# A hybrid attention and RWKV-7 layer: the recurrence's chain, norm and outputs split by group, one PSUM bank per step, and a new program order

## The chip, the cores and the metric

The kernel runs on one core of one Trainium2 chip. The time is device microseconds of one execution; the median of three runs stands for the kernel before. The core's engines each run their own queue of instructions in order: TensorE (PE, with its weight loads PEld), VectorE (DVE), ScalarE (ACT), GpSimd (POOL), and SyncE (SP), which here only starts DMAs. They wait for each other by semaphores.

## The reference

One layer on x of 1024 tokens by 1024 features: a norm, one large projection, then multi-head latent attention (MLA, 4 heads) and an RWKV-7 recurrence (8 heads of 64) side by side, gates z, an output projection and a second norm. Cut to what matters:

```python
u = rmsnorm(h, norm_pre_g[l])
p = u @ w_in[l]
p_mla, p_rw, z = jnp.split(p, [MLA_COLS, MLA_COLS + RW_SHIFT_COLS], axis=-1)
c_q, c_kv, k_r = jnp.split(p_mla, [Q_LORA, Q_LORA + KV_LORA], axis=-1)
q = (rmsnorm(c_q, mla_q_norm_g[l]) @ mla_w_uq[l]).reshape(B, T, MLA_HEADS, MLA_NOPE + MLA_ROPE)
kv = (rmsnorm(c_kv, mla_kv_norm_g[l]) @ mla_w_ukv[l]).reshape(B, T, MLA_HEADS, MLA_NOPE + MLA_V)
...
def step(S, inp):
    r_t, w_t, k_t, v_t, kk_t, a_t = inp
    sa = jnp.einsum('bhvk,bhk->bhv', S, -kk_t)
    S = (S * w_t[:, :, None, :] + sa[..., None] * (kk_t * a_t)[:, :, None, :]
         + v_t[..., None] * k_t[:, :, None, :])
    return S, jnp.einsum('bhvk,bhk->bhv', S, r_t)
```

The state S of the recurrence (64 by 64 for each head) goes from token to token. The recurrence's output is normed by head, gets a bonus term, and is gated like the attention's output.

## The kernel before

The tokens are done in two halves of 512. The operations are letters with the half and, where there is one, the block behind them, and `PROGRAM` is their list. A is the first norm and the transposes of x (into uH and uL, a value split in two parts of reduced precision). X is the low-rank input of the decay and of a, and P the projections of one block of 128 columns (two heads) for r, k and v: 24 matmuls each, by `proj` (L209). E builds the block's chunk matrices. Z is the projection of one block of the gates, again 24 matmuls, and Y of two. M and T are the input of the latent attention: M projects (L532 to L534), copies the result out (L544, on DVE), norms it, and T transposes it, multiplies by the norm's gain (L559, DVE) and sends it to DRAM (cTd).

The recurrence is done by chunks of 64 tokens, 8 to a half. I inverts the chunks' triangular 64 by 64 matrices: on DVE, 31 steps of a product and an add (L417, L419) for the 32 by 32 blocks on the diagonal, then a round trip through DRAM (sx, st), then products on TensorE (L446, L453) for the block below. C is the chain over the 8 chunks. A step has four products: R = LS(first half of the columns) x S (L467), Y = LS(second half) x S (L470), U = AB x R (L479) and the new state from BK x U (L484), to which DVE adds the decayed old state SD (L490), and a second part of Y (L486). R and U are copied out of PSUM by ScalarE (L473, L481), Y too (L492); SD is made by POOL (L476). All four column blocks with both heads of each go through a step together, 8 small matmuls for a product (each two passes). N norms the output by head (L500 to L506; L502 and L503 are a logarithm and an exponential on ScalarE with a load of its tables each), and loads the bonus (bvd) onto the squares' place. G transposes the result (L518), applies gain and bias (L520) and writes it to DRAM (yrw).

The attention: B makes the cos and sin tables (L661 to L672), U loads the up weights (w_uq, w_ukv) and cTd and splits each value in two parts (L625 to L628), K turns the key's rope part, Q computes the rotated queries of 256 tokens (L750 and on), J the first head's q and k, `values` (L811 to L815) the values of two heads. S is attention for 4 heads (scores L834, probabilities times values L866) and the output projection (L912).

What sets the order: the kernel is handed to a list scheduler, in which the order of `PROGRAM` is the priority. The order that it builds is fixed on each engine. Buffers bind it: PSUM is allotted by tags, four banks of 512 numbers "pj" (projections), two "wk" and two "ch" (the chain, the norm's transposes, the attention's output). In SBUF a tag is one buffer, or as many as `bufs` says, shared by all that ask for it in turn: "q" has two. A tensor SV of the first kernel holds state and output of all four blocks of a half in one buffer; the values and the final output use its place later. LS, BK and AB come two blocks ("group") to a buffer, with two buffers.

Of the kernel before, what the change touches and what calls it, by code (L numbers as in the profile page):

```python
# [44 lines left out]
def layer(tc, x, pos, w_in, w_out, w_uq, w_ukv, vecs, w2, a2, consts, post_g, out):  # L45
# [84 lines left out]
    "A0 X0 P00 E00 Z00 P01 E01 Z01 P02 E02 Z02 P03 E03 I0 M0 Z03 Z04 Z05 C0 Z06 Z07 T0 A1 X1 N0",  # L130
    "P10 G0 E10 Z10 P11 E11 Z11 P12 E12 Z12 P13 E13 I1 M1 Z13 Z14 T1 Z15 Z16 Z17 C1 U B K Q0 Q1 Q2 Q3 J N1 G1 S",
# [3 lines left out]
def recurrence(tc, E):  # L135
# [17 lines left out]
    def stage_a(h):  # L153

        XT = (("v", "sq"), ("sg", "cs"), ("a", "k"), ("kf", "r"))
        for pr in range(2):
            xs = []
            for q in range(2):
                t = h * 4 + pr * 2 + q
                xh = [alloc(P1, (128, 512), XT[pr * 2 + q][i]) for i in range(2)]  # L160
                ss = alloc(P1, (128, 2), "ss1", bufs=4)
                for i in range(2):
                    SP.dma_start(xh[i], x[t * 128:(t + 1) * 128, i * 512:(i + 1) * 512])
                    junk = alloc(P1, (128, 512), "q", BF16, bufs=2)
                    S.activation(junk, xh[i], AF.Square, accum_out=ss[:, i:i + 1])
                G.tensor_tensor(ss[:, 0:1], ss[:, 0:1], ss[:, 1:2], ALU.add)
                E["rstd"](ss[:, 0:1], 1.0 / D)
                for i in range(2):
                    V.tensor_scalar(xh[i], xh[i], ss[:, 0:1], 1.0, ALU.mult, ALU.mult)
                xs.append(xh)  # L170
            for k2 in range(4):
                ps = pj((128, 2, 256))
                for kk in range(2):
                    kb = k2 * 2 + kk
                    for q in range(2):
                        PE.transpose(ps[:, kk, q * 128:(q + 1) * 128], xs[q][kb // 4][:, (kb % 4) * 128:(kb % 4 + 1) * 128], ident)  # L176
# [90 lines left out]

    def prep(h, xx, cb, gt):
# [48 lines left out]
        rk = alloc(P1, (128, 512), "q", bufs=2)  # L317
# [139 lines left out]
    def chain(h, gt):  # L457

        SV, Dg = gt["SV"], gt["Dg"]
        LS, BK, AB = ([gt["g"][b // 2][k][:, b % 2] for b in range(4)] for k in ("LS", "BK", "AB"))  # L460
        be = [(b, e) for b in range(4) for e in range(2)]
        for e in range(2):
            G.tensor_copy(SV[ev[e], 0, e], Sst[ev[e]])
        for c in range(NCH):
            pR = chp((128, 4, 64))
            for b, e in be:
                PE.matmul(pR[ev[e], b], LS[b][:, c, e, 0:64], SV[:, c, e, b], start=True, stop=True)  # L467
# [5 lines left out]
            S.copy(Rs, pR)  # L473
# [4 lines left out]
            for b, e in be:
                PE.matmul(pU[ev[e], b], AB[b][ev[e], c, 0:64], Rs[ev[e], b], start=True, stop=True)  # L479
            for e in range(2):  # L480
                S.copy(SV[ev[e], c, e], pU[ev[e]])  # L481
# [1 line left out]
            for b, e in be:
                PE.matmul(pS[ev[e], b], BK[b][:, c, e], SV[:, c, e, b], start=True, stop=True)  # L484
            for b, e in be:
                PE.matmul(pY[ev[e], b], AB[b][ev[e], c, 64:128], SV[ev[e], c, e, b], start=False, stop=True,  # L486
                          skip_group_check=True)
            for e in range(2):
                dst = SV[ev[e], c + 1, e] if c + 1 < NCH else Sst[ev[e]]
                V.tensor_tensor(dst, pS[ev[e]], SD[ev[e]], ALU.add)  # L490

            S.copy(SV[:, c, 0], pY)  # L492

    def group_norm(h, gt):

        y, sq = gt["SV"][:, :, 0], gt["SV"][:, :, 1]
# [6 lines left out]
        S.activation(ss, ss, AF.Exp, scale=-0.5)  # L503
        for c4 in range(0, NCH, 4):
            cs = slice(c4, c4 + 4)
            V.tensor_tensor(y[:, cs], y[:, cs], bc(ss[:, cs].unsqueeze(3), (128, 4, 4, 64)), ALU.mult)  # L506
        for e in range(2):
            for b in range(4):
                SP.dma_start(sq[ev[b % 2], :, (b // 2) * 2 + e], bvd[h, b, ev[e]].rearrange("p (c t) -> p c t", t=64))

    def outputs(h, gt):

        for g in range(2):
            for e in range(2):
                o = gt["SV"][:, :, 1, 2 * g + e]
                pT = chp((128, NCH, 64))
                for c in range(NCH):
                    PE.transpose(pT[:, c], gt["SV"][ev[e], c, 0, 2 * g:2 * g + 2].rearrange("p l v -> p (l v)"),  # L518
                                 ident[ev[e], ev[e]])
                V.scalar_tensor_tensor(o, pT, hln[:, 2 * g + e:2 * g + e + 1], o, ALU.mult, ALU.add)  # L520
                b = (2 * g + e) * 128
                SP.dma_start(yrw[b:b + 128, h * HALF:(h + 1) * HALF].rearrange("p (c t) -> p c t", t=64), o)

    def mla_in(h):
# [11 lines left out]
        for t in range(4):  # L536
# [7 lines left out]
            V.tensor_copy(cq, pss[t][:, 0:384])  # L544
# [6 lines left out]
    def mla_tail(h, cqs):  # L551
        for t, (cq, ss) in enumerate(cqs):
# [6 lines left out]
            V.tensor_tensor(cT, ps, bc(vec[:, V_QG:V_QG + 3].unsqueeze(2), (128, 3, 128)), ALU.mult)  # L559
# [42 lines left out]
    def op_m(h):  # L602
# [10 lines left out]
def attention(tc, E):  # L613
# [16 lines left out]
    identr = causalr = sint = cost = sintq = costq = None  # L630
    cqH = cqL = ckH = ckL = uqH = uqL = ukH = ukL = krT = None

    def op_b():
# [37 lines left out]

        V.tensor_scalar_mul(tabq, tab, -SCALE)  # L672

    def op_u():
# [17 lines left out]
        for kb in range(2):  # L692
            for i in range(2):
# [358 lines left out]
```

## Time and profile before

| | |
|---|---|
| median of the three runs | 796.23 us |
| the runs | 796.23, 797.51, 792.93 us |
| the profiled execution | 792.52 us |
| its span in the profile | 790.7 us (1.8 us lie around it) |
| mean granted TensorE clock | 0.93 |

A row of the timeline gives the start in us, the length, engine, line, operation, the tiles written and read, and how many instructions of a kind it holds; in brackets stands how long the engine had been idle before it and what released it. In a table of groups the busy time, the mean ns of one, and the idle time ahead stand behind the bars. A row of windows gives for each engine the busy time in that stretch and the count of instructions, in the order PE, PEld, DVE, ACT, POOL, then the granted clock of TensorE, the share of time in which DMA engines were busy, and GB/s. Line numbers in these rows are those of the kernel before.

### The profile page before, as it was taken

Reading aid. Unit: us, or ns where it says so; the run is one execution under the profiler, and the core shown is the slowest. Engines: PE = TensorE matmul, PEld = TensorE weight load, DVE = VectorE, ACT = ScalarE, POOL = GpSimd, SP = SyncE. Lnnn points to the kernel's source line nnn. Section 1 sums busy time; section 2 is a strip of 40 time slices with the busy share of each in tenths; the row PEclk is TensorE's granted clock in tenths of the full one; section 3 lists DMA queues with packets and bytes.
Section 4 is the critical chain, followed back from the end, with each engine's and each line's share of the span. In section 5 each row is a group of like instructions: output and inputs, shape, how many; then the busy total and the mean of one; then the engine's idle time right before and its main releaser. Section 6 shows DMA issues by size and latency. Waiting matters only on the chain.

```text
span 790.7 us, 13588 instructions
## 1 busy us (share of the span) xinstructions
PE 694.5 (88%) x5088; PEld 577.1 (73%) x5088; DVE 458.5 (58%) x888; ACT 346.3 (44%) x825; POOL 304.5 (39%) x426
## 2 busy tenths in 40 slices
PE   3699999997988998879999968597579998899996
PEld 2478787886866777658888856486469997788884
DVE  5464755759735420684685785484356766644342
ACT  6445455335534462444443532345435566532221
POOL 6443645627632444133455541112102237332110
PEclk9799999998979899869999989699879999999998
DMA  7323223262480123152233434502130034154321
GB/s 208 103 55 87 71 71 109 80 191 73 149 194 27 47 88 80 35 121 52 64 88 80 116 115 135 159 14 64 45 70 14 22 101 146 52 169 133 120 80 53
DMA packets 118818, 72.83 MB, mean 92 GB/s; under 512 B 47072, under 2 KB 108256, under 8 KB 118752
## 3 DMA queue, kind: packets, MB, share of 16 engines
q1 hardware_dynamic: 118752, 71.96, 32.3%
q8 instruction: 40, 0.66, 0.3%
q14 instruction: 26, 0.21, 0.1%
HBM read 54.38 MB, written 17.56 MB: 91 GB/s over the span
## 4 chain that ended last, share of the span: by engine, by line
PE 63%; DVE 14%; DMA 8%; ACT 5%; issue 4%; SPq 3%; POOL 3%; DVEq 0%; ACTq 0%; POOLq 0%
PE pj L209 23%; PE pj L912 11%; PE wk L358 4%; PE pj L834 4%; PE ch L866 3%; PE wk L372 3%; DVE XA L419 2%; DVE tmp L417 2%; PE wk L855 1%; PE pj L176 1%; PE pj L532 1%; PE pj L383 1%; PE ch L484 1%; SPq L436 1%; PE pj L785 1%
## 5 line engine op out<-in xcount | busy, mean ns | idle before, releaser
L209 PE MATMUL pj<-uH,w 128*128 128x512 f32 x672 | 226.6, 413 | 13.2 <-DVE st L559 6.6
L199 POOL TENSOR_TENSOR w<-wf,w 128x256 fp32r<-128x256 f32 x168 | 140.0, 865 | 147.9 <-ACT w L189 138.8
L209 PEld LDWEIGHTS pj<-uH,w 128*128 128x128 f32 x672 | 130.4, 196 | 45.0 <-DVE st L559 6.8
L209 PE MATMUL pj<-uL,w 128*128 128x512 f32 x336 | 137.0, 408 | 0.0
L209 PEld LDWEIGHTS pj<-uL,w 128*128 128x128 f32 x336 | 66.1, 197 | 15.2 <-issue 1.0
L189 ACT CAST w<-wf 128x1024 fp32r<-128x1024 f32 (+1 forms) x50 | 51.3, 1025 | 22.1 <-PE pj L534 11.2
L846 POOL TENSOR_SCALAR wf<-wf,sm 128x128 f32<-128x128 f32 (+7 forms) x32 | 24.2, 759 | 90.0 <-DVE sm L845 74.6
L476 POOL TENSOR_TENSOR SD<-SV,Dg 64x256 f32<-64x256 f32 x32 | 21.8, 680 | 45.8 <-DVE SV L490 38.4
L866 PE MATMUL ch<-BK,SV 128*128 128x256 f32 (+1 forms) x160 | 33.4, 292 | 4.2 <-ACT SV L814 3.9
L358 PEld LDWEIGHTS wk<-LS,pl 64*128 64x128 f32 x256 | 27.2, 194 | 11.1 <-issue 9.0
L970 DVE TENSOR_TENSOR SV<-pj,SV 128x512 f32<-128x512 f32 x16 | 11.1, 691 | 41.6 <-ACT cq L969 40.7
L197 POOL TENSOR_TENSOR w<-wf,w 128x224 fp32r<-128x224 f32 x32 | 23.0, 749 | 29.3 <-ACT w L189 29.3
L857 ACT CAST BK<-wk 128x512 fp32r<-128x512 f32 (+3 forms) x48 | 22.5, 484 | 26.9 <-PE wk L855 24.6
L358 PE MATMUL wk<-LS,pl 64*128 64x128 f32 x256 | 32.3, 292 | 1.5 <-DVE LS L316 1.5
L490 DVE TENSOR_TENSOR SV<-ch,SD 64x256 f32<-64x256 f32 x28 | 11.8, 421 | 37.7 <-PE ch L484 37.3
L842 ACT ACTIVATE wf<-pj,mx 128x512 f32<-128x512 f32 (+3 forms) x48 | 27.9, 587 | 11.5 <-DVE mx L839 8.1
L566 ACT ACTIVATE st<-pj 128x512 f32<-128x512 f32 x16 | 9.6, 598 | 52.1 <-PE pj L209 38.6
L858 DVE TENSOR_TENSOR AB<-wk,BK 128x512 fp32r<-128x512 f32 (+3 forms) x48 | 26.1, 551 | 9.6 <-ACT BK L857 9.1
L837 DVE TENSOR_REDUCE mx<-pj 128x1 f32<-128x512 f32 (+3 forms) x48 | 25.8, 550 | 9.0 <-PE pj L836 5.0
L866 PEld LDWEIGHTS ch<-BK,SV 128*128 128x128 f32 x160 | 27.1, 200 | 4.9 <-ACT SV L814 4.1
L417 DVE TENSOR_TENSOR tmp<-XA 128x31 f32<-128x31 f32 (+15 forms) x62 | 27.2, 439 | 4.3 <-DMA XA<-sa 2.8
L372 PEld LDWEIGHTS wk<-r,pl 64*128 64x128 f32 x256 | 26.7, 189 | 2.8 <-issue 2.8
(332 smaller groups left out, 1595.8 us busy)
## 6 DMA issues: line engine op xcount, KB each, us to landing
wf<-in_w_in_dram SPq DMA_DIRECT2D x42, 512.0 KB, 3.9
zs<-st SPq DMA_DIRECT2D x16, 256.0 KB, 2.7
wf<-in_x_dram SPq DMA_DIRECT2D x8, 512.0 KB, 3.8
out_dram<-SV SPq DMA_DIRECT2D x16, 256.0 KB, 2.0
wf<-in_w_in_dram SPq DMA_DIRECT2D x8, 448.0 KB, 3.6
bvd<-st SPq DMA_DIRECT2D x8, 256.0 KB, 2.0
SV<-bvd SPq DMA_DIRECT2D x16, 128.0 KB, 2.9
yrw<-SV SPq DMA_DIRECT2D x8, 256.0 KB, 2.4
```

The source lines that it names most:

```text
L189: S.copy(wh, wf)
L199: G.tensor_tensor(wl[:, sl], wf[:, sl], wh[:, sl].bitcast(F32), ALU.subtract)
L209: PE.matmul(ps, w_[:, kb], u_[:, kb], start=(n == 0), stop=(n == 23))
L358: PE.matmul(pE[e][:, ci], pl[r, c4 + ci, 1 - e:3 - e].rearrange("p a b -> p (a b)"), LS[r, c4 + ci, e, :], start=True, stop=True)
L372: PE.matmul(pB[:, c], pl[r, c, 1 - e:3 - e].rearrange("p a b -> p (a b)"), dD[r, c], start=True, stop=True)
L417: V.tensor_tensor(t3, bc(At[:, j, j + 1:32].unsqueeze(2), (128, n, w)), bc(X[:, j, 0:w].unsqueeze(1), (128, n, w)), ALU.mult)
L834: PE.matmul(s_, l_, r_, start=(n == 0), stop=(n == 4 and b1 < e))
L837: V.tensor_reduce(mx[:, n5:n5 + 1], s_, axis=AX.X, op=ALU.min)
L842: S.activation(pr[:, b0:b1], sc[:, 0:b1 - b0], AF.Exp, bias=mx[:, 0:1], scale=-1.0, accum_out=sm[:, n5:n5 + 1])
L858: V.tensor_tensor(PL[:, b0:b0 + nb, o], pt[:, 0:nb], PH[:, b0:b0 + nb, o].bitcast(F32), ALU.subtract)
L866: PE.matmul(py[:, o], l_, r_, start=(j == 0 and n == 0), stop=(j == nk - 1 and n == 2), skip_group_check=True)
L912: PE.matmul(po[nb], l_, r_[:, ns], start=(k0 == 0 and k == 0 and n == 0), stop=(k0 == 4 and k == 3 and n == 2), skip_group_check=True)
```

## The change

The order of the program is new. Inverse, chain, norm and outputs of a half stand ahead of M of that half, Z00 ahead of P00, B at the end of the first half, and J ahead of Q.

`chain`, `group_norm` and `outputs` get a group g of two blocks, and a half calls them once for each group. R, Y, U and the new state of a step stand in one PSUM bank, four quarters of it. SV is one tensor for each group, with two buffers. The norm's root is a power on POOL. M's copy and T's copy are ScalarE's; the gains of the two latent norms are multiplied onto the up weights instead (`scaled`). The scale of the queries, formerly in tables of its own, is applied where the rotated queries are split. The tag "q" has one buffer.

```diff
 PROGRAM = (
-    "A0 X0 P00 E00 Z00 P01 E01 Z01 P02 E02 Z02 P03 E03 I0 M0 Z03 Z04 Z05 C0 Z06 Z07 T0 A1 X1 N0",
-    "P10 G0 E10 Z10 P11 E11 Z11 P12 E12 Z12 P13 E13 I1 M1 Z13 Z14 T1 Z15 Z16 Z17 C1 U B K Q0 Q1 Q2 Q3 J N1 G1 S",
+    "A0 X0 Z00 P00 E00 Z01 P01 E01 Z02 P02 E02 Z03 P03 E03 I0 C00 C01 N00 G00 N01 G01 M0 Z04 Z05 Y06 T0 A1 X1 B",
+    "P10 E10 Z10 P11 E11 Z11 P12 E12 Z12 P13 E13 I1 C10 C11 N10 G10 N11 G11 M1 Z13 T1 Z14 Z15 Z16 Z17 U K J Q0",
+    "Q1 Q2 Q3 S",
 )
...
+            SV=alloc(P1, (128, NCH, 2, 2, 64), "SV", bufs=2),
         ) for _ in range(2)]
         return dict(
             g=gs,
-            SV=alloc(P1, (128, NCH, 2, 4, 64), "SV", bufs=1),
...
-        rk = alloc(P1, (128, 512), "q", bufs=2)
+        rk = alloc(P1, (128, 512), "q")
...
-    def chain(h, gt):
+    def chain(h, g, gt):
...
         for c in range(NCH):
-            pR = chp((128, 4, 64))
-            for b, e in be:
-                PE.matmul(pR[ev[e], b], LS[b][:, c, e, 0:64], SV[:, c, e, b], start=True, stop=True)
-            pY = chp((128, 4, 64))
...
+            pc = chp((128, 4, 2, 64))
+            pR, pY, pU, pS = (pc[:, i] for i in range(4))
+            for l, e in le:
+                PE.matmul(pR[ev[e], l], LS[:, l, c, e, 0:64], SV[:, c, e, l], start=(l == 0), stop=False,
                           skip_group_check=True)
-            Rs = alloc(P1, (128, 4, 64), "Rs")
+            for l, e in le:
+                PE.matmul(pY[ev[e], l], LS[:, l, c, e, 64:128], SV[:, c, e, l], start=False, stop=False,
+                          skip_group_check=True)
+            Rs = alloc(P1, (128, 2, 64), "Rs", bufs=2)
             S.copy(Rs, pR)
...
-    def group_norm(h, gt):
+    def group_norm(h, g, gt):
...
-        S.activation(ss, ss, AF.Ln, bias=epst[:, 1:2], scale=1.0 / 64)
-        S.activation(ss, ss, AF.Exp, scale=-0.5)
+        G.tensor_scalar(ss, ss, 1.0 / 64, GN_EPS, ALU.mult, ALU.add)
+        G.tensor_tensor(ss, ss, bc(E["mhalf"][:, 0:1].unsqueeze(2), (128, NCH, 2)), ALU.pow)
...
-            V.tensor_copy(cq, pss[t][:, 0:384])
+            S.copy(cq, pss[t][:, 0:384])
...
-            V.tensor_tensor(cT, ps, bc(vec[:, V_QG:V_QG + 3].unsqueeze(2), (128, 3, 128)), ALU.mult)
+            S.copy(cT, ps)
...
+    def scaled(dst_h, dst_l, src, c):
+
+        G.tensor_scalar(dst_h, src, vec[:, c:c + 1], 1.0, ALU.mult, ALU.mult)
+        V.scalar_tensor_tensor(dst_l, src, vec[:, c:c + 1], dst_h.bitcast(F32), ALU.mult, ALU.subtract)
...
-                split(uqH[:, kb, sl], uqL[:, kb, sl], wf)
+                scaled(uqH[:, kb, sl], uqL[:, kb, sl], wf, V_QG + kb)
...
-        V.tensor_scalar_mul(tabq, tab, -SCALE)
...
-        S.copy(qs[:, :, 0].bitcast(F32R), qo)
-        V.tensor_tensor(qs[:, :, 1], qo, qs[:, :, 0], ALU.subtract)
+        S.activation(qs[:, :, 0].bitcast(F32R), qo, AF.Copy, scale=-SCALE)
+        V.scalar_tensor_tensor(qs[:, :, 1], qo, -SCALE, qs[:, :, 0], ALU.mult, ALU.subtract)
...
-            vt = own[0][:, 2 * e:2 * e + 2].rearrange("p s (k c) -> p s k c", c=128)
+            vt = alloc(P2, (128, 2, 8, 128), "SV", F32R, bufs=2)
```

Three places show how the built order moves. In the rows a name is a tile with its number, `ch_4839` a bank of the chain, and the last field gives the columns of the result and the count.

On TensorE the end of the second half's chain, before: the last full step of all four blocks (LS_2658 and LS_2661 are its two groups).

```order
L467 MATMUL ch_4830<-SV_2664,LS_2658 64x64 x4
L467 MATMUL ch_4830<-SV_2664,LS_2661 64x64 x4
L470 MATMUL ch_4839<-SV_2664,LS_2658 64x64 x4
L470 MATMUL ch_4839<-SV_2664,LS_2661 64x64 x4
L479 MATMUL ch_4853<-Rs_4848,AB_2660 64x64 x4
L479 MATMUL ch_4853<-Rs_4848,AB_2663 64x64 x4
L486 MATMUL ch_4839<-SV_2664,AB_2660 64x64
L484 MATMUL ch_4864<-SV_2664,BK_2659 64x64 x4
L484 MATMUL ch_4864<-SV_2664,BK_2662 64x64 x4
L486 MATMUL ch_4839<-SV_2664,AB_2660 64x64 x3
L486 MATMUL ch_4839<-SV_2664,AB_2663 64x64 x4
```

The same place now: two of the second group's half-steps, one bank each (LS_2869 is the second group; the first group's steps stand ahead of these).

```order
L469 MATMUL ch_4625<-SV_2872,LS_2869 64x64 x4
L472 MATMUL ch_4625<-SV_2872,LS_2869 64x64 x4
L480 MATMUL ch_4625<-Rs_4634,AB_2871 64x64 x4
L485 MATMUL ch_4625<-SV_2872,BK_2870 64x64 x4
L487 MATMUL ch_4625<-SV_2872,AB_2871 64x64 x4
L469 MATMUL ch_4656<-SV_2872,LS_2869 64x64 x4
L472 MATMUL ch_4656<-SV_2872,LS_2869 64x64 x4
L480 MATMUL ch_4656<-Rs_4665,AB_2871 64x64 x4
L485 MATMUL ch_4656<-SV_2872,BK_2870 64x64 x4
L487 MATMUL ch_4656<-SV_2872,AB_2871 64x64 x4
```

A step of four blocks has become two of two blocks; the groups follow one another, and in both kernels no other matmul stands between the rows of this place.

On DVE, in the middle of the second half's inverse (tmp and XA are its operands), before:

```order
L544 COPY cq_4210<-pj_4056 128x384
L661 TENSOR_SCALAR q_4976<-xw_4978 128x256 x2
L419 TENSOR_TENSOR XA_3789<-XA_3789,tmp_3826 128x20x12
L662 TENSOR_SCALAR xw_4978<-q_4976 128x256
L544 COPY cq_4222<-pj_4057 128x384
L417 TENSOR_TENSOR tmp_3829<-XA_3789 128x247
L663 TENSOR_TENSOR q_4976<-q_4976,xw_4978 128x256
L419 TENSOR_TENSOR XA_3789<-XA_3789,tmp_3829 128x19x13
```

The same steps of the inverse now:

```order
L418 TENSOR_TENSOR tmp_3990<-XA_3953 128x240
L420 TENSOR_TENSOR XA_3953<-XA_3953,tmp_3990 128x20x12
L418 TENSOR_TENSOR tmp_3993<-XA_3953 128x247
L420 TENSOR_TENSOR XA_3953<-XA_3953,tmp_3993 128x19x13
L418 TENSOR_TENSOR tmp_3996<-XA_3953 128x252
L420 TENSOR_TENSOR XA_3953<-XA_3953,tmp_3996 128x18x14
```

The copies of M and the table work of B have left DVE's queue between the inverse's operations.

On TensorE near the start, where the low-rank products (L249, L250) wait for their input, before:

```order
L209 MATMUL pj_247<-uL_99,w_241 128x512
L209 MATMUL pj_247<-uH_98,w_241 128x512
L249 MATMUL pj_294<-xw_279,lora_228 128x512
L250 MATMUL pj_294<-xw_279,lora_228 128x512
L249 MATMUL pj_301<-xa_280,lora_228 128x512
```

And now (pj_293 is Z00's bank):

```order
L210 MATMUL pj_293<-uH_98,w_287 128x512 x2
L210 MATMUL pj_293<-uL_99,w_287 128x512
L210 MATMUL pj_293<-uH_98,w_287 128x512
L250 MATMUL pj_331<-xw_279,lora_228 128x512
L251 MATMUL pj_331<-xw_279,lora_228 128x512
L250 MATMUL pj_338<-xa_280,lora_228 128x512
```

The 24 matmuls of Z00 now stand between the input's projection (pj_247) and the low-rank products.

More of the change, by code (lines that the diff above doesn't have):

```diff
@@ L477, in chain @@
-            pU = chp((128, 4, 64))
-            for b, e in be:
-                PE.matmul(pU[ev[e], b], AB[b][ev[e], c, 0:64], Rs[ev[e], b], start=True, stop=True)
+                G.tensor_tensor(SD[ev[e]], SV[ev[e], c, e], bc(Dg[ev[e], :, c:c + 1], (64, 2, 64)), ALU.mult)
+            for l, e in le:
+                PE.matmul(pU[ev[e], l], AB[ev[e], l, c, 0:64], Rs[ev[e], l], start=False, stop=False,
+                          skip_group_check=True)
             for e in range(2):
                 S.copy(SV[ev[e], c, e], pU[ev[e]])
-            pS = chp((128, 4, 64))
@@ L483, in chain @@
[L483 to L487, printed above, removed]
+            for l, e in le:
+                PE.matmul(pS[ev[e], l], BK[:, l, c, e], SV[:, c, e, l], start=False, stop=False, skip_group_check=True)
+            for l, e in le:
+                PE.matmul(pY[ev[e], l], AB[ev[e], l, c, 64:128], SV[ev[e], c, e, l], start=False,
+                          stop=True, skip_group_check=True)
@@ L501, in group_norm, with outputs @@
             V.tensor_reduce(ss[:, cs], sq[:, cs], axis=AX.X, op=ALU.add)
-        S.activation(ss, ss, AF.Ln, bias=epst[:, 1:2], scale=1.0 / 64)
-        S.activation(ss, ss, AF.Exp, scale=-0.5)
+        G.tensor_scalar(ss, ss, 1.0 / 64, GN_EPS, ALU.mult, ALU.add)
+        G.tensor_tensor(ss, ss, bc(E["mhalf"][:, 0:1].unsqueeze(2), (128, NCH, 2)), ALU.pow)
         for c4 in range(0, NCH, 4):
             cs = slice(c4, c4 + 4)
-            V.tensor_tensor(y[:, cs], y[:, cs], bc(ss[:, cs].unsqueeze(3), (128, 4, 4, 64)), ALU.mult)
-        for e in range(2):
[L508 to L522, printed above, removed]
+            V.tensor_tensor(y[:, cs], y[:, cs], bc(ss[:, cs].unsqueeze(3), (128, 4, 2, 64)), ALU.mult)
+        for l in range(2):
+            for e in range(2):
+                SP.dma_start(sq[ev[l], :, e], bvd[h, 2 * g + l, ev[e]].rearrange("p (c t) -> p c t", t=64))
+    def outputs(h, g, gt):
+        SV = gt["g"][g]["SV"]
+        for e in range(2):
+            o = SV[:, :, 1, e]
+            pT = chp((128, NCH, 64))
+            for c in range(NCH):
+                PE.transpose(pT[:, c], SV[ev[e], c, 0].rearrange("p l v -> p (l v)"), ident[ev[e], ev[e]])
+            V.scalar_tensor_tensor(o, pT, hln[:, 2 * g + e:2 * g + e + 1], o, ALU.mult, ALU.add)
+            b = (2 * g + e) * 128
+            SP.dma_start(yrw[b:b + 128, h * HALF:(h + 1) * HALF].rearrange("p (c t) -> p c t", t=64), o)
     def mla_in(h):
@@ L606, in recurrence @@
         "A": stage_a, "X": op_x, "P": op_p, "M": op_m, "T": lambda h: mla_tail(h, cqs[h]),
-        "E": op_e, "I": lambda h: inverse(h, gts[h]), "C": lambda h: chain(h, gts[h]),
-        "N": lambda h: group_norm(h, gts[h]), "G": lambda h: outputs(h, gts[h]), "Z": lambda h, b: zgate(h, b, b + 1),
+        "E": op_e, "I": lambda h: inverse(h, gts[h]), "C": lambda h, g: chain(h, g, gts[h]),
+        "N": lambda h, g: group_norm(h, g, gts[h]), "G": lambda h, g: outputs(h, g, gts[h]), "Z": lambda h, b: zgate(h, b, b + 1),
         "Y": zgate2,
@@ L616, in attention @@
     alloc, bc = E["alloc"], E["bc"]
-    hln, epst, ident, causal, invf = (E[k] for k in ("hln", "epst", "ident", "causal", "invf"))
+    hln, epst, ident, causal, invf, vec = (E[k] for k in ("hln", "epst", "ident", "causal", "invf", "vec"))
     x, pos, w_out, w_uq, w_ukv, post_g, out = (E[k] for k in ("x", "pos", "w_out", "w_uq", "w_ukv", "post_g", "out"))
@@ L920, in op_s @@
     def op_s():
-        own.append(alloc(P2, (128, 4, T), "SV", F32R, bufs=1))
         prs, pp = {}, {}
@@ L951, in op_s @@
         load_wo(0, 2, "LS", 2, V, G)
-        po_ = alloc(P2, (128, 4, D), "SV", bufs=1)
-        pg = po_[:, 0]
+        sv = [alloc(P2, (128, 2, D), "SV", bufs=2) for _ in range(2)]
+        pg, *rows = (v_[:, i] for v_ in sv for i in range(2))
         SP.dma_start(pg, post_g.partition_broadcast(128))
@@ L964, in op_s @@
             ss = alloc(P2, (128, 2), "oss", bufs=2)
-            o = po_[:, 1 + t % 3]
+            o = rows[t % 3]
             for nb in range(2):
```

43 lines of the change are left out of this document (19 added, 24 removed).

## The prediction

> **What bounds the kernel now.** I read the page first (engine totals, the chain that ended last), then the waits of the tensor engine one by one on the timeline, and last the granted clock in windows.
>
> ```profile
> PE 694.5 (88%) x5088; PEld 577.1 (73%) x5088; DVE 458.5 (58%) x888; ACT 346.3 (44%) x825; POOL 304.5 (39%) x426
> ```
>
> The tensor engine works in 694.5 of 790.7 us, so 96 us of idling are what a change of order can win or lose. The other engines matter only where it waits for them. The largest such places that the change touches are these:
>
> ```profile
> 34.30 0.77 PE L249 MATMUL pj<-xw,lora 128*128 128x512 f32 x1 [6.01 <-DVE xw L241]
> 192.22 0.79 PE L209 MATMUL pj<-uH,w 128*128 128x512 f32 x1 [5.05 <-DVE cq L544]
> 231.03 0.48 PE L176 MATMUL pj<-cst,v 128*128 128x128 f32 x1 [3.33 <-DVE st L559]
> 468.53 0.79 PE L209 MATMUL pj<-uH,w 128*128 128x512 f32 x1 [6.60 <-DVE st L559]
> 510.26 0.74 PE L750 MATMUL pj<-pl,uH 128*128 128x256 f32 x4 [0.76 <-POOL pl L627]
> ```
>
> Each row gives the start, the length, the operation and, in brackets, how long the engine had stood idle and for what. In the second, third and fourth the engine waits for DVE copies (L544, L559) that stand in DVE's queue among the operations of the inverse. The last row is the start of the attention products that fill the second chain. Four steps of that chain stand bare, with nothing else on the tensor engine; one of them, by engine:
>
> ```profile
> 555.75 0.69 PE L467 MATMUL ch<-SV,LS 128*64 128x64 f32 x16 [0.53 <-DVE SV L490]
> 556.47 0.37 ACT L473 COPY Rs<-ch 128x256 f32<-128x256 f32 x1 [0.79 <-PE ch L467]
> 556.89 0.68 PE L479 MATMUL ch<-Rs,AB 64*64 64x64 f32 x16
> 557.68 0.76 ACT L481 COPY SV<-ch 64x256 f32<-64x256 f32 x2 [0.84 <-PE ch L479]
> 558.49 0.69 PE L484 MATMUL ch<-SV,BK 128*64 128x64 f32 x16
> 559.29 0.88 DVE L490 TENSOR_TENSOR SV<-ch,SD 64x256 f32<-64x256 f32 x2 [3.69 <-PE ch L484]
> 560.31 0.69 PE L467 MATMUL ch<-SV,LS 128*64 128x64 f32 x16 [0.54 <-DVE SV L490]
> ```
>
> A full step is 560.31 - 555.75 = 4.56 us: a loop of latencies in which tensor engine, ScalarE, tensor engine, ScalarE, tensor engine and DVE follow each other, and no one of them is busy all the time. Behind the last one comes the tail:
>
> ```profile
> 564.44 0.37 ACT L492 COPY SV<-ch 128x256 f32<-128x256 f32 x1 [0.34 <-PE ch L486]
> 564.84 1.06 ACT L500 ACTIVATE SV<-SV 128x1024 f32<-128x1024 f32 x1
> 565.93 1.22 DVE L501 TENSOR_REDUCE gss<-SV 128x16 f32<-128x1024 f32 x1 [0.55 <-ACT SV L500]
> 569.47 2.36 DVE L506 TENSOR_TENSOR SV<-SV,gss 128x1024 f32<-128x1024 f32 x2 [1.86 <-ACT gss L503]
> 573.42 2.02 PE L518 MATMUL ch<-cst,SV 64*128 64x64 f32 x16 [0.83 <-DVE SV L520]
> 579.36 0.58 PE L866 MATMUL ch<-BK,SV 128*128 128x256 f32 x1 [3.92 <-ACT SV L814]
> 581.14 1.22 PE L834 MATMUL pj<-w,w 128*128 128x512 f32 x2 [0.21 <-DVE SV L815]
> ```
>
> From the last chain copy to the next scores (L834) it is 16.7 us. L518, the output transposes, runs at 573.42 and L866 then waits for values whose buffer the outputs have to leave first. Behind 581 the order of the work is the same in both kernels, and so is its length. The question is therefore when L834 comes.
>
> **The sum up to the second inverse.** The gate projection Z00, 24 matmuls, now stands in the 6.01 us of the low-rank gap, and M0's and T0's copies leave DVE's queue for ScalarE's, so 5.05 and 3.33 go too: 14.4 us. Against that stand three bare half-steps in the first half (below: 3.7 us each, 1.8 of it matmul, so 5.7 idle), where the end of the old chain idled a little too, and a wait ahead of the block E12. I give 4.4 back in all, an estimate between 0 and 8. So the second inverse starts **10** earlier (6 to 14). The chain's matmuls, the preparation and the gate projections are as many as before; they only change places.
>
> **Second inverse.**
>
> ```profile
> L419 DVE TENSOR_TENSOR XA<-XA,tmp 128x31 f32<-128x31 f32 (+15 forms) x31 | 12.9, 416 | 0.7
> L417 DVE TENSOR_TENSOR tmp<-XA 128x31 f32<-128x31 f32 (+15 forms) x31 | 12.8, 413 | 1.5 <-DMA XA<-sa 0.9
> L559 DVE TENSOR_TENSOR st<-pj,vec 128x384 f32<-128x384 f32 x4 | 2.2, 554 | 1.8 <-DMA zs<-st 1.3 <-DMA cTd<-st 0.5
> L544 DVE COPY cq<-pj 128x384 f32<-128x384 f32 x4 | 2.2, 550 | 0.0
> L665 DVE TENSOR_TENSOR q<-q,xw 128x256 f32<-128x256 f32 x2 | 1.4, 686 | 0.0
> L666 DVE TENSOR_SCALAR q<-q 128x256 f32<-128x256 f32 x2 | 1.1, 551 | 0.0
> L672 DVE TENSOR_SCALAR q<-q 128x512 f32<-128x512 f32 x1 | 1.0, 965 | 0.6 <-ACT q L667 0.6
> 509.21 1.00 POOL L627 TENSOR_SCALAR pl<-cq 128x384 fp32r<-128x384 f32 x2 [26.89 <-DMA cq<-in_w_uq_dram]
> ```
>
> The first two groups are the 62 operations of the inverse itself; L559, L544 and the table work of B (L661 to L672) stand between them in DVE's order and leave it: 2.2 + 1.8 + 2.2 + 1.4 + 1.1 + 1.0 + 0.6 = 10.3, say **11** with B's smaller ones. ScalarE takes the eight copies and is 44% busy; if it were late, who would wait is the transposes of the tail T, at most 8 x 0.55 = 4.4. SyncE's queue still holds the inverse's round trip through DRAM ahead of the loads of the up weights, so the POOL pass at 509.21 and the first product at 510.26 keep their distance from the inverse's end, and come 10 + 11 = 21 earlier: the fill starts at **489**. The gains folded into the weights keep the count and shapes of the passes: 0, bounds 0 and 1.
>
> **Fill.** Products and chain share these 36.2 us (second row: the chain's tiles alone):
>
> ```profile
> 510.20:546.40 36.20, 32.95 (x415) 28.14 (x415) 26.52 (x63) 17.62 (x61) 8.02 (x17) 1.00 0.19 57
> 510.20:546.40 36.20, 12.11 (x272) 9.98 (x272) 3.35 (x8) 5.14 (x14) 1.00 0.19 57
> ```
>
> The number behind the length is PE's busy time. Other work is 32.95 - 12.11 = 20.8, idle time 3.2. The new order has five half-steps between these products, about 1.8 of matmul each: 20.8 + 9 + 3.2 = 33, ending at **522**. The projection banks are then held by values whose copies wait for a buffer that only the second group's outputs free, so there is nothing more to fill with.
>
> **Bare half-steps.** The groups run one after the other; 10.2 half-steps are bare (one pair overlaps), where 4 full ones were. Small copies:
>
> ```profile
> L857 ACT CAST BK<-wk 128x128 fp32r<-128x128 f32 x8 | 2.2, 275 | 1.0 <-PE ch L484 0.6 <-PE wk L855 0.3
> L858 DVE TENSOR_TENSOR AB<-wk,BK 128x128 fp32r<-128x128 f32 x8 | 2.3, 285 | 0.1
> ```
>
> In the loop the first copy now waits for R and Y in the shared bank, 8 + 8 passes, as many as the 16 before: 0.72 + 0.32; U with 8 passes 0.50; two small copies 0.60; S and the second half of Y, 16 passes, 0.80; two adds and the start 0.72. That is **3.7** (3.4 if ScalarE and DVE overlap better, 4.56 if nothing shrinks). Behind the waiting copy stand only this group's own SV copies. Then the clock: each half-step has 16 + 8 + 16 passes, some 1.8 us of 3.7, a busy share of 0.49.
>
> ```profile
> 553.43:556.84 3.41, 2.71 (x64) 2.32 (x64) 0.84 (x2) 1.16 (x4) 1.08 (x2) 1.00 0.00 0
> 652.40:655.81 3.41, 1.95 (x11) 1.54 (x10) 2.98 (x6) 2.47 (x7) 2.52 (x2) 1.00 0.60 186
> 317.85:321.25 3.40, 1.90 (x47) 1.63 (x44) 2.73 (x4) 1.53 (x4) 0.80 (x2) 1.00 0.00 0
> 321.28:324.69 3.41, 3.41 (x17) 2.97 (x15) 0.94 (x2) 1.86 (x5) 1.68 (x3) 0.50 0.01 2
> 236.39 1.12 PE L467 MATMUL ch<-SV,LS 128*64 128x64 f32 x16
> ```
>
> The third number from the right is the granted clock. Bare full steps, busy 0.79, keep 1.00. A stretch at 0.57 keeps it, but after the one at 0.56 that ends the first chain the clock stands at 0.50 though the engine is full. Half-steps at 0.49 lie below both. At half clock 16 passes take 1.12 instead of 0.69: +0.43 for R and Y, +0.2 for U, +0.43 behind it, so 4.75. The clock could cost from 0 to 10.2 x 1.06 = 10.8; by the nearest row I take half clock for nine of 10.2: 10.2 x 3.7 + 9 x 1.06 = 47.3, ending at 569.3. Before, the four bare steps took 4 x 4.56 = 18.2: here the change gives back what its earlier start brings.
>
> The new POOL power (L504) stands in one step's way; nearest rows:
>
> ```profile
> L58 POOL TENSOR_TENSOR mss<-mss,mhalf 128x2 f32<-128x2 f32 x8 | 6.2, 786 | 0.3
> L58 POOL TENSOR_TENSOR ss<-ss,mhalf 128x1 f32<-128x1 f32 x8 | 4.9, 606 | 0.4
> ```
>
> The difference of the two is 0.18 per column, so 16 columns are 0.43 + 16 x 0.18 = 3.3 (0.8 if columns cost nothing, 5 if the step is dearer). One step is late by 2: chain end **571.3**.
>
> **Tail.** Copy 0.4, half squares 0.6, half reduce 0.6, POOL 0.5 + 3.3, products 1.3, half the transposes 1.4, one output add 0.75, mix 1.8 as before: **10.7**. The two table loads of the norm are gone, and so is the wait ahead of L866, since the first head's values now lie in the first group's buffer, which is free by then. L834 at 571.3 + 10.7 = 582.0, before 581.1: +0.9. Half clock in half of the three bare half-steps of the first half: +1.6. **Sum +2.5** on the profiled run of 792.5 (its span plus 1.8): 795.0. That run lies 3.7 under the median of 796.2, so 798.7.
>
> Single-buffered q tiles I take at 0 (bounds 0 and 4, about one wait as long as the 3.33 above): the matmul that reads one stands well ahead of the next block's write, and the projections between hide it.
>
> **The rivals.**
> *The clock holds.* The bare half-steps take 3.7: 795.0 - 9.5 - 1.6 = 784, on the median's scale 788. For it: pauses in a half-step stay below 1 us, and 0.57 kept the clock once. Against it: the row at 321.28, after pauses no longer than 1.5. The Trainium skill's "TensorE: Matmul & The Clock Gate", section "What's actually happening", has the clock fall after a whole idle window of about 3.4 us; by that rule this rival would win. Its section "A second HAM failure mode: psum-queue depth-cycling" says that frequent short pauses can make it swing, which is my forecast; the trace sides with that.
> *All goes well.* Besides, half-steps of 3.4 (-3), a fill from 485 (-4), a power of 1 us (-4): 773, or 777 on the median's scale.
> *Slower: the preparation of the second half starves.* E12 needs the second group's LS buffer, which the first half's last half-step frees; P12's and P13's projections now all stand ahead of E12.
>
> ```profile
> 389.00:412.00 23.00, 23.00 (x131) 18.85 (x130) 19.57 (x35) 11.41 (x19) 13.06 (x16) 0.93 0.26 70
> ```
>
> In this window of the old preparation, about a block, DVE works 19.6 us beside 131 matmuls in 23.0. The three projections of a block are 72 of these, so with them gone 10.4 us of matmul would stand beside 19.6 of DVE: 9 idle per block, twice, less about 4 already counted: up to +14. With half to all of it, +7 to +14: 806 to 813 on the median's scale. It decides if the chain ends after P13's projections; against it, DVE can do part of P12 and P13 early.
>
> **How the numbers follow.** Forecast 0.48 (own range 792 to 807), the clock holds 0.20, all goes well 0.10, starved 0.22. About 0.5%, 4 us, is what a measurement of this kernel can tell. Faster: 0.10 + 0.17 + 0.05 of the forecast's low end = 0.32. Same: 0.25 + 0.03 = 0.28. Slower: 0.18 + 0.22 = 0.40. The range 780 to 811 leaves out most of "all goes well" and the tail of the starved case.
>
> **What would show it.** Right: granted clock 0.50 under bare half-steps about 4.7 apart, ten of them; the first attention product near 489; 11 us from the last chain copy to the scores. Wrong: half-steps of 3.7 at 1.00; an inverse that starts less than 6 or more than 14 earlier; an idle tensor engine around E12; a power far from 3.3.

## The result, and the profile after

The changed kernel takes 847.74 us (median of four runs, 844.57 to 852.22), the one before 795.36 beside it: a ratio of 1.066, 95% interval 1.060 to 1.073. It is 52 us slower, where the prediction gave 798.7 and a range up to 811. The profiled execution took 852.22 us, with a span of 850.4.

The page of the changed kernel, busy times and two of the rows by fortieths of the span:

```profile
PE 748.2 (88%) x5136; PEld 616.6 (73%) x5136; DVE 458.4 (54%) x911; ACT 360.3 (42%) x903; POOL 325.0 (38%) x470
...
PE   3899999999589989999978986987648998989996
...
PEclk9999999999778977799968987695558999999999
```

The tensor engine does the same products (48 more matmuls are recorded because the last two gate blocks are projected in tiles half as wide) and is busy 54 us longer. Its idle time grew by only 6 us (850.4 - 748.2 = 102.2, before 96.2). What grew is the time at a lower granted clock: the mean over the span fell from 0.930 to 0.881, and 1 less the mean, times the span, is 55 us before and 101 after. Not all of these 46 us are lost, since the engine also idles in them. A busy share alone would have hidden this: at half clock the same matmul counts as busy for longer.

The joints of the path, in us from the start of the span (the last column is a version from the experiments below):

| | before | changed | with turns |
|---|---|---|---|
| first product of the first chain | 236.4 | 234.3 | 232.7 |
| first product of E10 | 320.8 | 316.8 | 320.8 |
| first product of E12 | 389.2 | 424.9 | 384.2 |
| second inverse starts | 438.9 | 473.1 | 432.3 |
| first attention product | 510.3 | 536.7 | 501.1 |
| last chain copy | 564.4 | 626.0 | 557.7 |
| first scores after the chain | 581.1 | 640.2 | 574.9 |
| end of the span | 790.7 | 850.4 | 784.8 |

At E10 the changed kernel is level in time but not in work. From the first chain product to E10 it did 540 matmuls, where the kernel before did 815 in about the same time (82.5 and 84.4 us, at a granted clock of 0.83 and 0.94): the second group's chain was still to come. Between E10 and E12 it falls 40 us behind. The tensor engine is busy there for 105.1 of 108.1 us, with that chain and with projections that stood behind E12 before. It makes up 9 us from E12 to the first attention product, and from there to the last chain copy it falls behind by another 35.

The next rows are of the changed kernel: the Y product of the first half's last half-step, DVE where the LS buffer of the block E12 is first written (L310), and the tensor engine at E12.

```profile
411.31 0.40 PE L472 MATMUL ch<-SV,LS 128*64 128x64 f32 x8
...
411.76 2.05 DVE L310 SCALAR_TENSOR_TENSOR LS<-k,vec,sg 64x512 f32<-64x512 f32 x2 [4.96 <-PE ch L472]
...
424.88 1.71 PE L359 MATMUL wk<-LS,pl 64*128 64x128 f32 x16
430.08 1.19 PE L359 MATMUL wk<-LS,pl 64*128 64x128 f32 x4 [3.49 <-DVE LS L364]
```

DVE waits for L472, the last reader of that buffer. In the kernel before, the same write stood at 374 and shows no wait:

```profile
374.16 1.50 DVE L309 SCALAR_TENSOR_TENSOR LS<-k,vec,sg 64x512 f32<-64x512 f32 x2
```

The windows from E12's first product to the second inverse, changed kernel first, then before (PE busy behind the length, granted clock third from the right):

```profile
424.90:473.10 48.20, 39.56 (x229) 35.41 (x229) 26.82 (x44) 16.02 (x42) 13.75 (x22) 0.75 0.29 74
```

```profile
389.20:438.90 49.70, 49.70 (x294) 42.12 (x294) 33.45 (x57) 20.76 (x42) 25.89 (x35) 0.97 0.33 93
```

The stretch is as long as before, though 65 matmuls of it had been done ahead: the engine idles 8.6 us, runs at 0.75, and waits for the copies of its own blocks.

From the first chain product to the second inverse the two kernels do nearly the same matmuls (1484 recorded, 1466 before). The changed kernel takes 238.8 us for them, the one before 202.5. Of the 36.3 us between them, 30.3 are longer busy time, at a granted clock of 0.83 throughout (0.94 up to E10 and 0.88 behind it before), and 6.0 are idle time.

The bare half-steps, on the tensor engine of the changed kernel: one at full clock, then one at half clock.

```profile
572.87 0.71 PE L469 MATMUL ch<-SV,LS 128*64 128x64 f32 x7 [0.46 <-DVE SV L491]
...
574.23 0.45 PE L480 MATMUL ch<-Rs,AB 64*64 64x64 f32 x8 [0.35 <-ACT Rs L475]
575.37 0.45 PE L485 MATMUL ch<-SV,BK 128*64 128x64 f32 x8 [0.70 <-ACT SV L483]
...
576.66 0.70 PE L469 MATMUL ch<-SV,LS 128*64 128x64 f32 x4 [0.46 <-DVE SV L491]
...
604.25 0.91 PE L469 MATMUL ch<-SV,LS 128*64 128x64 f32 x7 [0.46 <-DVE SV L491]
...
606.04 0.69 PE L480 MATMUL ch<-Rs,AB 64*64 64x64 f32 x8 [0.36 <-ACT Rs L475]
607.44 0.70 PE L485 MATMUL ch<-SV,BK 128*64 128x64 f32 x8 [0.70 <-ACT SV L483]
...
609.21 0.47 PE L469 MATMUL ch<-SV,LS 128*64 128x64 f32 x2 [0.46 <-DVE SV L491]
```

From L469 to L469 it is 3.79 us in the first and 4.96 in the second. The waits for other engines in the brackets are the same to 0.01; only the products are longer (8 passes of L480: 0.45 and 0.69). The clock fell at 576.8. The 3.41 us ahead of that, with the engine busy for 1.90 us and no pause above 0.70:

```profile
573.43:576.84 3.41, 1.90 (x40) 1.42 (x36) 0.49 (x2) 0.87 (x4) 0.50 (x2) 1.00 0.00 0
```

The tail after the last half-step, by start, all engines:

```profile
625.95 0.27 ACT L493 COPY SV<-ch 128x128 f32<-128x128 f32 x1 [0.94 <-DVE Sst L491]
...
628.05 2.90 POOL L504 TENSOR_TENSOR gss<-gss,mhalf 128x16 f32<-128x16 f32 x1
...
631.81 1.21 PE L519 MATMUL ch<-cst,SV 64*128 64x64 f32 x16 [6.70 <-DVE SV L507]
633.95 0.55 PE L868 MATMUL ch<-BK,SV 128*128 128x256 f32 x1 [0.92 <-DVE SV L520]
639.33 1.20 ACT L816 CAST SV<-pj 128x256 fp32r<-128x256 f32 x4 [10.94 <-DMA yrw<-SV]
640.22 1.22 PE L836 MATMUL pj<-w,w 128*128 128x512 f32 x2 [4.76 <-DVE SV L817]
```

The first mix (L868) comes 8.0 us after the chain's last copy, but the scores (L836) need a projection bank. These are held by the second head's values until the output DMA (yrw) has left their buffer.

### The profile page after: what moved, and what is told of

Same layout as the page of the kernel before. It is cut to its first block, busy times and chain, and to the rows that moved or that the text cites. A ratio compares the mean times of both kernels' runs of the same rounds, so it can differ in the third digit from the quotient of the medians.

```text
span 850.4 us, 13845 instructions
## 1 busy us (share of the span) xinstructions
PE 748.2 (88%) x5136; PEld 616.6 (73%) x5136; DVE 458.4 (54%) x911; ACT 360.3 (42%) x903; POOL 325.0 (38%) x470
## 4 chain that ended last, share of the span: by engine, by line
PE 31%; DVE 8%; ACT 4%; DMA 4%; issue 2%; POOL 1%; SPq 1%; DVEq 0%; ACTq 0%; POOLq 0%
PE pj L914 10%; PE pj L836 4%; PE ch L868 3%; PE pj L210 3%; PE wk L857 1%; PE pj L788 1%; PE ch L469 1%; DVE XA L420 1%; DVE tmp L418 1%; PE ch L485 1%; PE ch L487 1%; PE ch L480 1%; PE pj L752 1%; PE pj L795 1%; POOL gss L504 1%
## 5 line engine op out<-in xcount | busy, mean ns | idle before, releaser
L210 PE MATMUL pj<-uH,w 128*128 128x512 f32 x640 | 219.5, 418 | 3.2 <-DVE uL L182 1.5
L210 PEld LDWEIGHTS pj<-uH,w 128*128 128x128 f32 x640 | 125.5, 198 | 34.8 <-DVE uL L182 1.9
L210 PE MATMUL pj<-uL,w 128*128 128x512 f32 x320 | 131.4, 411 | 0.0
L478 POOL TENSOR_TENSOR SD<-SV,Dg 64x128 f32<-64x128 f32 x64 | 28.1, 439 | 80.5 <-DVE SV L491 77.3
L491 DVE TENSOR_TENSOR SV<-ch,SD 64x128 f32<-64x128 f32 x56 | 16.2, 288 | 69.6 <-PE ch L487 67.9
L359 PE MATMUL wk<-LS,pl 64*128 64x128 f32 x256 | 37.7, 305 | 4.0 <-DVE LS L364 3.5
L469 PE MATMUL ch<-SV,LS 128*64 128x64 f32 x256 | 23.9, 288 | 14.6 <-DVE SV L491 10.0
L868 PE MATMUL ch<-BK,SV 128*128 128x256 f32 (+1 forms) x160 | 33.4, 291 | 1.2 <-DVE SV L520 0.9
L469 PEld LDWEIGHTS ch<-SV,LS 128*64 128x64 f32 x256 | 17.8, 179 | 22.4 <-DVE SV L491 13.0
L493 ACT COPY SV<-ch 128x128 f32<-128x128 f32 x32 | 8.5, 266 | 58.3 <-DVE SV L491 49.1
L373 PE MATMUL wk<-r,pl 64*128 64x64 f32 x256 | 32.5, 296 | 0.3 <-DVE LS L364 0.3
```

The lines of the kernel that those rows point to most:

```text
L210: PE.matmul(ps, w_[:, kb], u_[:, kb], start=(n == 0), stop=(n == 23))
L359: PE.matmul(pE[e][:, ci], pl[r, c4 + ci, 1 - e:3 - e].rearrange("p a b -> p (a b)"), LS[r, c4 + ci, e, :], start=True, stop=True)
L373: PE.matmul(pB[:, c], pl[r, c, 1 - e:3 - e].rearrange("p a b -> p (a b)"), dD[r, c], start=True, stop=True)
L469: PE.matmul(pR[ev[e], l], LS[:, l, c, e, 0:64], SV[:, c, e, l], start=(l == 0), stop=False, skip_group_check=True)
L868: PE.matmul(py[:, o], l_, r_, start=(j == 0 and n == 0), stop=(j == nk - 1 and n == 2), skip_group_check=True)
```

## The experiments

Two theories stood against each other. A: the split into groups costs the time, because half-steps one after the other leave the tensor engine half empty (half clock), and because the second group's chain ends so late in the first half that E12 starves. B: the new program order costs it. For the bare steps there was a third, C: they cost latency whatever the clock.

**The groups in turn.** The chain becomes a generator, and the two groups' steps are written one after the other, a step of each in turn (C0 takes the place of C00 C01 in the list, C1 of C10 C11):

```diff
             S.copy(SV[:, c, 0], pY)
+            yield
...
-        "E": op_e, "I": lambda h: inverse(h, gts[h]), "C": lambda h, g: chain(h, g, gts[h]),
+        "E": op_e, "I": lambda h: inverse(h, gts[h]), "C": lambda h: list(zip(chain(h, 0, gts[h]), chain(h, 1, gts[h]))),
```

> The changed kernel, but the steps of the two groups written in turn (first group's step, second group's step), so that the scheduler has both chains in flight; all else as changed. Theory A (the loss is the serial half-steps: tensor engine half empty, granted clock 0.50, and a second chain that ends so late in the first half that the block E12 starves): a pair of half-steps takes about 4.6 us at 1.00, E12's first product comes 30 us earlier, and the kernel takes 785 to 805 us. Theory B (the new program order costs the time): 830 us or more.

Measured: 785.1 us, ratio 0.985 (0.979 to 0.990). This is A, and it is also faster than the kernel before. Its bare steps on the tensor engine, and the window around them:

```profile
547.66 0.45 PE L469 MATMUL ch<-SV,LS 128*64 128x64 f32 x8 [0.39 <-ACT SV L493]
...
548.42 0.45 PE L469 MATMUL ch<-SV,LS 128*64 128x64 f32 x8
...
552.17 0.45 PE L469 MATMUL ch<-SV,LS 128*64 128x64 f32 x8 [0.40 <-ACT SV L493]
```

```profile
535.00:558.00 23.00, 18.12 (x369) 14.20 (x368) 8.23 (x25) 12.49 (x45) 6.98 (x17) 1.00 0.01 2
```

Both groups take a step in 552.17 - 547.66 = 4.51 us, where two half-steps at half clock took 9.9. The engine is busy 0.79 of the time and keeps 1.00. E12 starts at 384.2, 41 us earlier, where 30 were expected.

**The split in the old order.** The changed code with the list of the kernel before (C00 C01 in the place of C0, N and G likewise):

> The changed kernel's code with the order of the kernel before (chain, norm and outputs still split by group, first group then second). Theory A: bare half-steps of 4.9 to 5.0 us at 0.50 and a late second chain remain, 830 to 860 us. Theory B: 790 to 805 us.

Measured: 857.75 us, ratio 1.077 (1.071 to 1.082). The loss stays without the new order, and is 10 us larger (856.76 to 860.58 in its runs, 844.57 to 852.22 for the change): with serial groups the new order helps.

**The new order without the split.** The kernel before with the new order as far as its buffers allow: B stays ahead of K, and the second half's norm and outputs stay late.

```diff
-    "A0 X0 P00 E00 Z00 P01 E01 Z01 P02 E02 Z02 P03 E03 I0 M0 Z03 Z04 Z05 C0 Z06 Z07 T0 A1 X1 N0",
+    "A0 X0 Z00 P00 E00 Z01 P01 E01 Z02 P02 E02 Z03 P03 E03 I0 C0 N0 G0 M0 Z04 Z05 Y06 T0 A1 X1",
...
+    "P10 E10 Z10 P11 E11 Z11 P12 E12 Z12 P13 E13 I1 C1 M1 Z13 T1 Z14 Z15 Z16 Z17 U B K J Q0",
+    "Q1 Q2 Q3 N1 G1 S",
```

> The code of the kernel before (all four blocks in a step) with the new order as far as its buffers allow: Z00 first, inverse and chain ahead of M, J ahead of Q; B stays ahead of K and the norm and outputs of the second half stay late. Theory A: no half-steps, so no loss; the shorter inverses count: 775 to 797 us. Theory B: 830 us or more.

Measured: 794.12 us, ratio 1.000 (0.997 to 1.003). In this form the order by itself neither costs nor gains; B falls.

**The clock by itself.** The second group's half-steps of the second half do some products again, into the chain's other bank, while they wait. The results are not read.

```diff
+            again = h == 1 and g == 1
+            if again:
+                w = chp((128, 4, 2, 64))
+                for l, e in le:
+                    PE.matmul(w[ev[e], 0, l], LS[:, l, c, e, 0:64], SV[:, c, e, l], start=True, stop=True)
...
+            if again:
+                for i in range(2):
+                    for l, e in le:
+                        PE.matmul(w[ev[e], 1 + i, l], AB[ev[e], l, c, 0:64], Rs[ev[e], l], start=True, stop=True)
...
+            if again:
+                for i in range(2):
+                    for l, e in le:
+                        PE.matmul(w[ev[e], 2 * i + 1, l], BK[:, l, c, e], SV[:, c, e, l], start=True, stop=True)
```

> The changed kernel with idle products added to the second group's half-steps of the second half: R, U and the state's product are done again into the chain's other bank, once, twice and twice, where the step waits for copies. It adds 20 small matmuls to a half-step and a wait for the bank's last copy (about 0.35 us). Theory A (the granted clock): the clock stays at 1.00 there, half-steps take 4.0 to 4.4 us instead of 4.97, and the time falls by 4 to 10 us. Theory C (the half-steps are only latency, the clock a symptom): they take 5.0 us or more, time the same or up to 5 us longer.

Measured: 842.91 us, ratio 1.057 (1.052 to 1.063), against 1.066 for the change. A step of this kernel on the tensor engine (L478, L490 and L501 are the added products; L485 is U, L494 the state):

```profile
603.06 0.50 PE L469 MATMUL ch<-SV,LS 128*64 128x64 f32 x7
...
603.65 0.43 PE L478 MATMUL ch<-SV,LS 128*64 128x64 f32 x7
604.36 0.45 PE L485 MATMUL ch<-Rs,AB 64*64 64x64 f32 x8 [0.28 <-ACT Rs L480]
604.64 0.63 PE L490 MATMUL ch<-Rs,AB 64*64 64x64 f32 x16
...
606.27 0.68 PE L501 MATMUL ch<-SV,BK 128*64 128x64 f32 x14
607.01 0.50 PE L469 MATMUL ch<-SV,LS 128*64 128x64 f32 x7
```

And the bare steps by windows, the changed kernel and then this one:

```profile
588.60:624.40 35.80, 25.16 (x289) 20.21 (x288) 7.36 (x18) 8.00 (x29) 8.39 (x16) 0.50 0.10 22
```

```profile
595.00:616.00 21.00, 19.77 (x446) 16.54 (x442) 4.08 (x13) 6.31 (x23) 4.79 (x12) 1.00 0.01 3
```

With twice the products a half-step takes 3.79 to 3.95 us, not 4.96, at 1.00 instead of 0.50. So C falls as the whole account: the useless work pays for itself, and about 1.1 us of a bare half-step are the clock. Latency is still the larger part. Two half-steps one after the other take 9.92 us at half clock and 7.58 at full clock, and the pair in turn takes 4.51, so a pair loses some 3.1 us to standing in a row and 2.3 to the clock. Nine bare half-steps at 1.17 each would be some 11 us of the 52 for the clock, an estimate. In this kernel the first group's bare steps still run at 0.50 (575 to 585), and the whole time fell by 4.8 only, with intervals that overlap.

**Which half costs what.** The turns in one half only:

> The groups' steps in turn in the first half only; the second half's groups one after the other as in the change. If the two losses are separate, this one takes away the starved block E12 and keeps the bare half-steps at the end: by the two traces the second inverse starts 473 - 432 = 41 us earlier, so 803 to 812 us. Rival: the second half's serial groups are the whole loss, or need the late start: 830 us or more.

> The groups' steps in turn in the second half only. If the two losses are separate, E12 still starves and the bare half-steps at half clock are gone: from the second inverse to the scores the changed kernel takes 167 us and the one with turns in both halves 142.5, so 24.5 less, 819 to 828 us. Rival: below 812, the late chain of the first half costs little by itself.

Measured: 815.52 us with turns in the first half (1.025, 1.021 to 1.030), 819.85 with turns in the second (1.030, 1.026 to 1.034). The first lies above its expected range: its second inverse does come 43 us earlier (at 430.4), but from there to the scores it takes 171 us, not 167. The two losses are separate and of like size. Against 785.1 with turns in both, the first half's serial groups cost 34.8 and the second half's 30.4, 65 together; the change lies 62.6 above 785.1. Where the first half is serial, E12's first write waits 4.96 for L472, and E12 starts at 422.6 (turns in the second half only) or 426.1 (old order); where it has turns, E12 starts at 384 (388 in the old order). That the buffer, and not only the late chain, is what holds E12 is the reading of that wait; a third buffer was not tried.

**The copies alone.** The kernel before with M's and T's copies on ScalarE and the gains in the up weights:

```diff
-            V.tensor_copy(cq, pss[t][:, 0:384])
+            S.copy(cq, pss[t][:, 0:384])
...
-            V.tensor_tensor(cT, ps, bc(vec[:, V_QG:V_QG + 3].unsqueeze(2), (128, 3, 128)), ALU.mult)
+            S.copy(cT, ps)
...
-            split(ukH[:, sl], ukL[:, sl], wf)
+            scaled(ukH[:, sl], ukL[:, sl], wf, V_KVG)
```

> The kernel before with one part of the change alone: M's and T's copies on ScalarE and the gains folded into the up weights. If DVE's queue between the inverse's operations counts, the inverse of the second half ends 4 to 6 us earlier and the time falls to 789 to 793 us. Rival: ScalarE is late instead, or another wait takes its place: 794 to 798 us.

Measured: 790.36 us, ratio 0.994 (0.991 to 0.997). This part of the change is a small gain. The second inverse lasts 38.5 us there (436.8 to 475.3), 42.8 before (438.9 to 481.7).

**Turns in the old order, and turns without the copies.**

> The changed code with the groups' steps in turn in both halves, but in the program order of the kernel before. If the order is worth as little here as with full steps (ratio 1.000), 784 to 790 us. Rival: the new order is what makes the version with turns faster than the kernel before: 793 us or more.

> The version with turns in both halves, with M's and T's copies back on DVE and the gains applied there (as before the change). Alone these moves were worth 0.62%. If they are worth as much here, 788 to 791 us; if M behind the inverse and chain hides them, 784 to 787.

The second puts the three edits of the copies back into the version with turns. Measured: 784.69 us, ratio 0.984 (0.978 to 0.990), and 790.4, ratio 0.995 (0.992 to 0.999). The order is worth nothing with turns either, and of the 1.5% that the version with turns gains, about 1 is due to the copies. Both times lie within the expected ranges.

**The norm's power.** In the version with turns the two groups' powers follow each other on POOL:

```profile
558.59 2.91 POOL L505 TENSOR_TENSOR gss<-gss,mhalf 128x16 f32<-128x16 f32 x1
...
562.37 3.21 POOL L505 TENSOR_TENSOR gss<-gss,mhalf 128x16 f32<-128x16 f32 x1
```

The second group's went to ScalarE:

```diff
+        if g == 0:
+            G.tensor_scalar(ss, ss, 1.0 / 64, GN_EPS, ALU.mult, ALU.add)
+            G.tensor_tensor(ss, ss, bc(E["mhalf"][:, 0:1].unsqueeze(2), (128, NCH, 2)), ALU.pow)
+        else:
+            S.activation(ss, ss, AF.Ln, bias=epst[:, 1:2], scale=1.0 / 64)
+            S.activation(ss, ss, AF.Exp, scale=-0.5)
```

> The version with turns in both halves, with the second group's norm by logarithm and exponential on ScalarE (as before the change) while the first group's power stays on POOL. If the two powers one after the other (2.91 and 3.21 us) hold the tail, its scores come 2 to 4 us earlier: 780 to 784 us, ratio 0.979 to 0.983. Rival: ScalarE's two table loads and what stands behind them take the place: 784 to 788.

Measured: 783.29 us, ratio 0.988 (0.983 to 0.992). The interval overlaps that of the version with turns (0.979 to 0.990): whether it helps is not settled. The time lies in the expected range, the ratio above it. The two table loads of 1.28 us take most of what the power took.

## Why the prediction was wrong, step by step

The prediction put the scores at 582.0; they came at 640.2. The 58 us are these:

- **The second inverse 10 us earlier (6 to 14).** Wrong, and this is the step that failed: it came 34.2 later (438.9 to 473.1), and with it everything behind it. Both terms of its sum were off. The 14.4 us of waits were counted as won, but the first chain started only 2.1 earlier (236.4 to 234.3). At the places named 1.72 and 1.47 us of waiting are left, but the engine now waits 4.29 and 3.06 us for the first inverse (at 218 and 226), which it had covered with other work, and E00 came 2.1 later, behind the 24 matmuls of Z00. The 4.4 given back became 36.3. The step took three bare half-steps and let the other work move along freely. In the trace the second group's chain came almost wholly behind E10, built between the projections of the second half, one half-step every 8 to 17 us, and its last half-step began at 411. Its LS buffer held E12 until then.
- **The rival that the preparation starves** had the mechanism and the place: the wait on L472, P12's and P13's projections ahead of E12, the idle engine around E12. It got a chance of 0.22 and a price of 7 to 14. The first half's serial groups cost 34.8 in the runs, of which the starved block is one part; the other is the chain that was only half done at E10. How the 34.8 us divide between the two was not measured. The price had only the idle time; behind E12 the clock is at 0.75 too, and the work done ahead did not shorten that stretch.
- **The inverse 11 us shorter.** In the changed kernel it takes 35.0 (473.1 to 508.1) for 42.8, so 7.8. The groups named did leave. Part of the difference is a wait that was not there before, for the key's rope part, ahead of L735, and one more copy of 0.7 (L374) that falls into the stretch; the rest is not singled out:

```profile
L735 DVE TENSOR_TENSOR xw<-a,tab 128x256 f32<-128x256 f32 x2 | 1.9, 939 | 1.3 <-DMA a<-krd 1.3
```

- **The distance from there to the first attention product** was kept at 28.6 and measured 28.6 (508.1 to 536.7): right. With the two steps above the fill starts 47.7 later than predicted.
- **The fill, 33 us** (with five half-steps in it): 36.2, 3 too little.
- **Bare half-steps, 3.7 us at full clock and 4.75 at half.** 3.79 and 4.96, and the clock fell as forecast from the rows of the first chain's end: 0.50 from 576.8 to the chain's end. The chain's end came 53.1 us after the fill (572.9 to 626.0), predicted 49.3. This part was right, and the rival in which the clock holds was wrong. The margin was thinner than the prediction thought: it reckoned a half-step busy by 0.49, below both of its rows, but by the profile's count the one from 572.87 to 576.66 is busy for 2.28 of 3.79 us, 0.60, above the row of 0.57 that kept its clock. Only the 3.41 us right ahead of the fall come to 0.56, the share of the row that lost it. So that the clock fell in the first bare half-steps was partly luck.

  The rule of the Trainium skill that the rival named ("TensorE: Matmul & The Clock Gate", section "What's actually happening"), a whole idle window before the clock falls, does not agree with these steps, whose pauses ahead of the fall stay below 1 us. The Trainium skill's section "A second HAM failure mode: psum-queue depth-cycling" on the same page, by which frequent short pauses can make the clock swing, agrees in that short pauses were enough; but here the clock did not swing back while the chain ran.
- **The power, 3.3 us:** 2.90, with 0.2 for the operation ahead of it. Right; half-steps around it took 5.7 instead of 5.0, so it delayed one by 0.8.
- **The tail, 10.7 us:** 14.3. The mix came after 8.0, but the step overlooked that the scores behind it need a bank which the second head's values hold until the outputs have left.

47.7 + 3.2 + 3.8 + 3.5 = 58.2, the whole difference. The start of the second inverse alone is 44.2 of it, three quarters. The range did not reach it because the step was priced from idle time, as the prediction's opening has it (96 us of idling are what a change of order can win or lose): idle time grew by 6 us and busy time by 54.

## What to carry to other kernels

A chain bound by latency should have its independent parts in flight together: when it is split into groups, write their steps in turn. Written one group behind the other, the second group's first step here began only beside the first group's last (314 and 313 us), as two banks given out in program order would have it; more banks were not tried. When a part of the work is delayed, follow the buffers that it reads to whoever writes them next, and price the stretch behind at the clock that a half-empty tensor engine got in such a place (0.75 behind E12). A joint that is reached in time says nothing of the work left behind it: count the matmuls too. To see where time went, compare 1 less the granted clock beside the idle time, stage by stage; the busy share was 88% in both kernels.

## What the runs showed of the hardware

- Twice the matmuls made a step shorter: 3.79 to 3.95 us with the added products, 4.96 without, at a granted clock of 1.00 and 0.50.
- The clock fell with no long pause: after 3.41 us in which the engine was busy by 0.56 and no pause was above 0.70 us. It then stayed at 0.50 through bare half-steps busy by 0.70 (25.16 of 35.80 us). With both groups in turn, busy 0.79, it stayed at 1.00 for 23 us.
- A power of 128x16 took 2.90 to 3.21 us on POOL, where 128x1 took 0.61 and 128x2 0.79: some 0.16 to 0.18 us a column by these figures, an estimate.
